# A gated convolution and state-space block on eight cores: the recurrence scanned over chunks of eight tokens, the convolution as banded products, and orders from a list scheduler

## The chip, the cores and the metric

The kernel runs on all 8 cores of one Trainium2 chip, one batch element per core. The metric is the device time of the slowest core, in microseconds (us). Some executions fall into a slower state, in which the cores of one die show a lower granted TensorE clock than those of the other (in the slowest run of e12, 2099.60 us, 0.803 against 0.969); such runs are called slow and are left out of every comparison. Several chips were used, so each changed kernel was timed in turns with the kernel before on the same chip.

Names: TensorE (PE in the profile) does matrix products, VectorE (DVE) and ScalarE (ACT) do elementwise work, and the DMA queues are issued by SyncE (SP) and GpSimd (POOL). PEld in the profile is the loading of a matrix into TensorE. "ps" names the banks of PSUM, the memory into which TensorE writes its sums. A table load (ACT_TABLE_LOAD) is an instruction in ScalarE's queue, 1283 ns each; it stands between some pairs of ScalarE functions and not between others. An eviction is the operation that takes a finished sum out of PSUM.

## The reference, cut to what matters

x is 8 x 2048 x 2048; 16 meta tokens are put in front, so each core works on 2064 tokens of width 2048. E is 1024.

```python
xn = rmsnorm(h)                                    # over 2048 channels
v, g, z_c, u, z_s, gl_c, gl_s = split(xn @ w_in)   # widths E,E,E,E,E,2048,2048
# convolution branch
a = v * sigmoid(g)
a = causal_depthwise_conv(a, width=31) + dw_b
y_c = silu(layernorm(a)) * silu(z_c)               # layer norm over the E channels
# state-space branch: 64 groups of 16 channels, 64 complex states per group
s[t] = lam_bar * s[t-1] + B_bar @ u[t]             # complex, diagonal lam_bar
y_s = gelu(real(C @ s) + d_skip * u)
y_s = y_s * sigmoid(y_s @ w_glu + b_glu) * silu(z_s)
# gated merge
m = sigmoid(gl_c + b) * (y_c @ w_conv) + sigmoid(gl_s + b) * (y_s @ w_ssm)
out = rmsnorm(h + m @ w_out)
```

Layer norm needs all 1024 channels of the convolution, and the products with `w_conv`, `w_ssm` and `w_out` come after both branches.

## The kernel before

Weights and activations are in bf16, sums in fp32. The text of the program is the order of each engine's queue; waits on semaphores are derived from the buffers that an operation reads and writes. A Python generator interleaves the recurrence with the projections by hand.

The recurrence works token by token on 512 tokens at a time, with two groups' 64 states on the 128 partitions. The complex state is turned into two real scans: the input is modulated by cosine and sine tables, scanned with a real decay, and demodulated again. All of that is VectorE's work (`S5ENG` is VectorE).

```python
# per pair of groups and tile of 512 tokens; f[0..3] are quarters of P and Q   (cut)
mm(ps[pr][:, 0:w], BT[rp:rp + 32, 0, blk, :], ub, ...)            # real part of B u
mm(ps[pi_][:, 0:w], BT[rp:rp + 32, 1, blk, :], ub, ...)           # imaginary part
tt("dve", Pv, psW, ecb, ALU.mult, ...)                            # modulation, 1024 wide
tt("dve", Qv, psW, esb, ALU.mult, ...)                            # modulation, 1024 wide
tt(S5ENG, f[0][:, 0:w], f[0][:, 0:w], f[1][:, 0:w], ALU.add, ...)
tt(S5ENG, f[2][:, 0:w], f[2][:, 0:w], f[3][:, 0:w], ALU.subtract, ...)
# ... two scans of 512, real and imaginary: tensor_tensor_scan(mult, add)
tt("dve", TT_["P"]..., SQ, ecb, ALU.mult, ...)                    # demodulation, 1024 wide
tt("dve", TT_["Q"]..., SQ, esb, ALU.mult, ...)                    # demodulation, 1024 wide
# ... then four products with C and one with the skip matrix on TensorE
```

The convolution has 23 of its 31 taps on TensorE, as products with diagonal matrices, and 8 taps on VectorE:

```python
for k in range(NDT, CW):                 # NDT = 8, CW = 31
    mm(ps[bk][:, 0:w], DG[m % 2][:, k - NDT, :], ABUF2[:, m, t0 + k:t0 + k + w], ...)
# ...
for k in range(1, NDT):
    for ai_, (t0, w) in enumerate(pair_tiles):
        stt(cacc[ai_][:, 0:w], ABUF2[:, m, t0 + k:t0 + k + w], dww_t[:, m, k:k + 1],
            cacc[ai_][:, 0:w], ALU.mult, ALU.add, ...)
```

Of the kernel before, what the change touches and what calls it, by code (L numbers as in the profile page):

```python
# [10 lines left out]
I32 = mybir.dt.int32  # L11
# [10 lines left out]
PADL = CW - 1  # L22
NORM_EPS = 1e-6
LN_EPS = 1e-5
SMW = 4352
# [4 lines left out]
TT_ALL = [(0, NM)] + [(NM + 512 * i, 512) for i in range(4)]  # L30
TT_REAL = TT_ALL[1:]

C_V, C_G, C_ZC, C_U, C_ZS, C_GLC, C_GLS = 0, 1024, 2048, 3072, 4096, 5120, 7168

SAME_ENGINE_WAITS = ("pool", "act", "dve")
S5ENG = "dve"

class _Stop(Exception):
    pass

class Src:
    def __init__(self, sem, step):
        self.sem, self.step, self.count = sem, step, 0

class Buf:
    __slots__ = ("w", "r")

    def __init__(self):
        self.w = None
        self.r = []  # L50

def alias_from(new_bufs, old_bufs):
    evs = []
    for b in old_bufs:
        if b.w is not None:
            evs.append(b.w)
        evs.extend(b.r)
    for nb in new_bufs:
        nb.r = list(nb.r) + evs

class Sched:
    def __init__(self):
        self.eng = {}

    def add_engine(self, name, sem):
        self.eng[name] = dict(src=Src(sem, 1), insts=[], waited={})

    def op(self, eng, fn, reads=(), writes=(), signal=True, src=None):
        En = self.eng[eng]
        s = src if src is not None else En["src"]  # L70
        need = {}
        srcs = {}
        deps = []
        for b in reads:
            if b.w is not None:
                deps.append(b.w)
        for b in writes:
            if b.w is not None:
                deps.append(b.w)
            deps.extend(b.r)  # L80
        for (ds, v) in deps:
            if ds is En["src"] and (eng == "pe" or eng not in SAME_ENGINE_WAITS):
                continue
            k = id(ds)
            if v > need.get(k, 0):
                need[k] = v
                srcs[k] = ds
        waits = []
        for k, v in need.items():
            if En["waited"].get(k, 0) >= v:  # L90
                continue
            En["waited"][k] = v
            waits.append((srcs[k].sem, v))
        if signal:
            s.count += s.step
            ev = (s, s.count)
            sig = (s.sem, s.step)
        else:
            ev = (s, s.count + s.step)
            sig = None  # L100
        En["insts"].append((waits, fn, sig))
        for b in reads:
            b.r.append(ev)
        for b in writes:
            b.w = ev
            b.r = []
        return ev

    def wait_all(self, eng, events):
        En = self.eng[eng]  # L110
        waits = []
        for (ds, v) in events:
            k = id(ds)
            if En["waited"].get(k, 0) >= v:
                continue
            En["waited"][k] = v
            waits.append((ds.sem, v))
        En["insts"].append((waits, None, None))

    def emit(self, name, e):  # L120
        for waits, fn, sig in self.eng[name]["insts"]:
            for sem, v in waits:
                e.wait_ge(sem, v)
            if fn is None:
                continue
            ins = fn(e)
            if sig is not None:
                ins.then_inc(sig[0], sig[1])

def build(dbg=None):  # L130
    nc = bass.Bass("TRN2", target_bir_lowering=False)
    S = Sched()
# [7 lines left out]
    w_in = din("w_in", [D, 9216])  # L140
    b_gate = din("b_gate", [4096])
    dw_w = din("dw_w", [CW, 1, E])
    dw_b = din("dw_b", [E])
    ln_g = din("ln_g", [E])
    ln_b = din("ln_b", [E])
    w_conv = din("w_conv", [E, D])
    lam_re = din("lam_re", [64, 64])
    lam_im = din("lam_im", [64, 64])
    log_step = din("log_step", [64])
    b_re = din("b_re", [64, 64, 16])  # L150
    b_im = din("b_im", [64, 64, 16])
    c_re = din("c_re", [64, 16, 64])
    c_im = din("c_im", [64, 16, 64])
    d_skip = din("d_skip", [E])
    w_glu = din("w_glu", [E, E])
    b_glu = din("b_glu", [E])
    w_ssm = din("w_ssm", [E, D])
    w_out = din("w_out", [D, D])
    final_g = din("final_g", [D])
    out = nc.dram_tensor("out", [SEQ, D], F32, kind="ExternalOutput").ap()  # L160
    ps_scr = nc.dram_tensor("ps_scr", [64, 128, L], BF16).ap()
    dbg_out = None
    if dbg is not None:
        dbg_out = nc.dram_tensor("dbg", list(dbg["shape"]), F32, kind="ExternalOutput").ap()

    es = ExitStack()
    with es:
        def sb(name, shape, dt):
            return es.enter_context(nc.sbuf_tensor(name, list(shape), dt))

        def sem(name):
            return es.enter_context(nc.semaphore(name))

        XM = sb("XM", [128, 16, L], BF16)
        AC = sb("AC", [128, 33264], BF16)
        WS = sb("WS", [128, 4, 4096], BF16)
        TA = sb("TA", [128, 8192], BF16)
        SM = sb("SM", [128, SMW], F32)
        ident = sb("ident", [128, 128], BF16)
        identf = sb("identf", [128, 128], F32)  # L180
        ones_b = sb("ones_b", [128, 128], BF16)
        BT = sb("BT", [128, 2, 8, 128], BF16)
        WC = sb("WC", [128, 3, 8, 128], BF16)
        DSKD = sb("DSKD", [128, 8, 128], BF16)
        ps2 = [es.enter_context(nc.psum_tensor(f"ps{i}", [128, 1024], F32)) for i in range(4)]
        ps = [ps2[j // 2][:, (j % 2) * 512:(j % 2 + 1) * 512] for j in range(8)]
        psB = [Buf() for _ in range(8)]

        A_EL = 8 * (L + PADL)
        Aap = AC[:, 0:A_EL]  # L190
        Cap = AC[:, A_EL:A_EL + 8 * L]
        ABUF = Aap.rearrange("p (b t) -> p b t", b=8)
        UBUF = ABUF[:, :, PADL:]
        CBUF = Cap.rearrange("p (b t) -> p b t", b=8)
        A_f32 = Aap.bitcast(F32)
        C_f32 = Cap.bitcast(F32)
        AC_f32 = AC[:, :].bitcast(F32)

        for n in ("pe", "act", "dve", "pool", "sp"):
            S.add_engine(n, sem("s_" + n))  # L200

        def dsrc(name):
            return Src(sem(name), 16)

        XMB = [[Buf() for _ in range(5)] for _ in range(16)]

        def tidx(t0):
            return 0 if t0 < NM else 1 + (t0 - NM) // 512

        def xm_all(k):  # L210
            return tuple(XMB[k])
        WSb = [Buf() for _ in range(4)]
        Ab = [Buf() for _ in range(8)]
        Cb = [Buf() for _ in range(8)]
        TAb = Buf()
        SMb = Buf()
        CONSTb = Buf()
        S5Wb = Buf()

        sm_off = [0]  # L220

        def smalloc(n):
            o = sm_off[0]
            sm_off[0] += n
            assert sm_off[0] <= SMW - 1024, sm_off[0]
            return SM[:, o:o + n]

        def act(out_, in_, func, bias=0.0, scale=1.0, accum=None, reads=(), writes=()):
            if accum is None:
                return S.op("act", lambda e: e.activation(out=out_, in_=in_, func=func, bias=bias, scale=scale),  # L230
                            reads, writes)
            return S.op("act", lambda e: e.activation(out=out_, in_=in_, func=func, bias=bias, scale=scale,  # L232
                                                      accum_out=accum), reads, writes)

        def tt(eng, out_, in0, in1, op, reads=(), writes=()):
            return S.op(eng, lambda e: e.tensor_tensor(out=out_, in0=in0, in1=in1, op=op), reads, writes)  # L236

        def ts(eng, out_, in0, s1, s2, op0, op1=None, reads=(), writes=()):
            if op1 is None:
                return S.op(eng, lambda e: e.tensor_scalar(out=out_, in0=in0, scalar1=s1, scalar2=None, op0=op0),  # L240
                            reads, writes)
            return S.op(eng, lambda e: e.tensor_scalar(out=out_, in0=in0, scalar1=s1, scalar2=s2, op0=op0, op1=op1),
                        reads, writes)

        def stt(out_, in0, scalar, in1, op0, op1, reads=(), writes=()):
            return S.op("dve", lambda e: e.scalar_tensor_tensor(out=out_, in0=in0, scalar=scalar, in1=in1,  # L246
                                                                op0=op0, op1=op1), reads, writes)

        def cp(eng, out_, in_, reads=(), writes=()):
            if eng == "act":  # L250
                return S.op("act", lambda e: e.copy(out=out_, in_=in_), reads, writes)  # L251
# [975 lines left out]
```

## Time and profile before

The kernel before took 2489.11 us (median of three runs, 2469.27 to 2709.86; the highest is a slow one).

| Reading | Value |
|---|---|
| span of the profiled core | 2464.5 us |
| TensorE busy | 2035.2 us (83%), 9368 matmuls |
| VectorE busy | 1732.1 us (70%) |
| ScalarE busy | 779.3 us (32%), 61 table loads |

The first view of the kernel before is the table by stages: the window in us and its length, then the busy time of each engine with its number of instructions, the granted TensorE clock (1.00 is full), the share of time in which the DMA engines were busy, and what they moved in GB/s.

```profile
core 2: us, PE busy (x) PEld busy (x) DVE busy (x) ACT busy (x) POOL busy (x), PEclk, DMA share, GB/s
0.00:246.00 246.00, 91.31 (x659) 56.04 (x660) 54.94 (x56) 64.77 (x93) 23.39 (x27) 0.89 0.61 96
246.00:400.00 154.00, 99.01 (x437) 44.32 (x435) 56.77 (x137) 42.75 (x98) 5.39 (x6) 0.79 0.19 24
400.00:1500.00 1100.00, 1074.62 (x4985) 437.73 (x4984) 1076.38 (x1468) 476.83 (x725) 33.11 (x29) 0.98 0.31 57
1500.00:1660.00 160.00, 108.28 (x444) 44.37 (x442) 58.97 (x65) 55.04 (x100) 1.18 (x2) 0.82 0.22 57
1660.00:1870.00 210.00, 174.09 (x748) 74.69 (x749) 194.35 (x297) 61.88 (x146) 1.75 (x2) 0.93 0.19 55
1870.00:2050.00 180.00, 122.08 (x471) 49.48 (x469) 123.22 (x177) 41.45 (x44) 4.38 (x5) 0.81 0.36 86
2050.00:2464.50 414.50, 365.80 (x1633) 161.21 (x1630) 167.51 (x218) 36.58 (x49) 7.88 (x9) 0.92 0.48 128
```

The middle stage, 400 to 1500 us, holds the recurrence and most projections. TensorE and VectorE are both about 98% busy there. The stages around it (start, 1500 to 1660, 1870 to 2050) leave TensorE idle for 155, 52 and 58 us.

The second view of the kernel before is TensorE's list of waits: what it waited for, in us in total, how often, and the longest.

```profile
PE ps L262 <- DVE AC L246: 148.4, 17, 28.7
PE ps L256 <- DVE XM L236: 70.3, 13, 23.8
PE ps L256 <- DMA AC<-w_out: 38.4, 8, 19.9
...
```

Its first line is the normalised x: TensorE waits for VectorE at the start. The third view, of the same kernel, is the chain of waits that ended last (start, duration, what); it shows the rate of dense matmuls of 512 columns, 7.01/32 = 219 ns and 210.42/968 = 217 ns.

```profile
391.18 7.01 PE ps L256 x32
...
2243.81 210.42 PE ps L256 x968
```

The fourth view of the kernel before is VectorE's groups by line and shape (busy us, mean ns of one). With the groups cut here (additions 166.1, the second scan 161.0, the other demodulation 98.9), modulation, demodulation, scans and taps make 1250 of VectorE's 1732 us.

```profile
L236 DVE TENSOR_TENSOR AC<-ps,TA 128x1024 f32<-128x1024 f32 x256 | 307.7, 1209 | 11.2 <-PE ps L258 11.0
L236 DVE TENSOR_TENSOR AC<-AC,TA 128x1024 bf16<-128x1024 f32 x172 | 202.5, 1218 | 0.1
...
L719 DVE TENSOR_TENSOR_SCAN AC<-SM,AC 128x512 f32<-128x512 f32 x128 | 163.8, 1280 | 6.5
...
L246 DVE SCALAR_TENSOR_TENSOR XM<-XM,SM 128x512 f32<-128x512 bf16 x224 | 149.7, 745 | 0.0
```

### The profile page before, as it was taken

Reading aid. Unit: us, or ns where it says so; the run is one execution under the profiler, and the core shown is the slowest. Engines: PE = TensorE matmul, PEld = TensorE weight load, DVE = VectorE, ACT = ScalarE, POOL = GpSimd, SP = SyncE. Lnnn points to the kernel's source line nnn. Section 1 sums busy time; section 2 is a strip of 40 time slices with the busy share of each in tenths; the row PEclk is TensorE's granted clock in tenths of the full one; section 3 lists DMA queues with packets and bytes.
Section 4 is the critical chain, followed back from the end, with each engine's and each line's share of the span. In section 5 each row is a group of like instructions: output and inputs, shape, how many; then the busy total and the mean of one; then the engine's idle time right before and its main releaser. Section 6 shows DMA issues by size and latency. Waiting matters only on the chain.

```text
span 2464.5 us, 27461 instructions; the slowest of 8 cores (2447.9 to 2464.5 us)
## 1 busy us (share of the span) xinstructions
PE 2035.2 (83%) x9368; PEld 867.8 (35%) x9368; DVE 1732.1 (70%) x2416; ACT 779.3 (32%) x1253; POOL 77.1 (3%) x80
## 2 busy tenths in 40 slices
PE   1056829998998999999999999558887749958998
PEld 1033414433333334444444444223333214423443
DVE  2122039999999999999999999129996767622333
ACT  3122133244443444535444443342323210001111
POOL 2100000000000000000000000000000000010000
PEclk9987959999999999999999999779988879977999
DMA  9831042323232323333233320231111264267444
GB/s 190 50 90 52 1 52 43 69 45 60 35 61 44 61 59 54 69 61 67 45 69 69 60 52 26 43 110 62 35 38 31 87 135 109 72 120 142 161 147 137
DMA packets 120953, 179.45 MB, mean 73 GB/s; under 512 B 6593, under 2 KB 96705, under 8 KB 114400
## 3 DMA queue, kind: packets, MB, share of 16 engines
q0 software_dynamic: 92848, 57.89, 20.4%
q1 hardware_dynamic: 27968, 119.81, 14.4%
q8 instruction: 77, 1.26, 0.2%
q14 instruction: 60, 0.49, 0.1%
HBM read 183.91 MB, written 50.40 MB: 95 GB/s over the span
## 4 chain that ended last, share of the span: by engine, by line
PE 67%; DVE 12%; DMA 8%; issue 8%; ACT 3%; another core or an unknown queue 1%; POOL 0%; DVEq 0%; SPq 0%; ACTq 0%; POOLq 0%
PE ps L256 59%; PE ps L258 7%; DVE AC L236 4%; DMA WS<-w_in 2%; DMA AC<-w_out 2%; DVE XM L236 2%; DMA AC<-x 1%; DVE AC L722 1%; DVE AC L246 1%; DMA TA<-ps_scr 1%; ACT TA L232 1%; DVE SM L236 1%; DMA WS<-ps_scr 1%; DVE AC L719 1%
## 5 line engine op out<-in xcount | busy, mean ns | idle before, releaser
L256 PE MATMUL ps<-XM,WS 128*128 128x512 bf16 (+1 forms) x4992 | 1047.5, 367 | 14.6 <-DMA WS<-w_in 6.3
L256 PEld LDWEIGHTS ps<-XM,WS 128*128 128x128 bf16 x4992 | 453.3, 99 | 591.0 <-issue 91.2
L256 PE MATMUL ps<-AC,WS 128*128 128x512 bf16 x1280 | 299.5, 399 | 80.5 <-DMA WS<-w_conv 30.5
L236 DVE TENSOR_TENSOR AC<-ps,TA 128x1024 f32<-128x1024 f32 (+1 forms) x320 | 316.1, 1002 | 14.2 <-PE ps L258 11.0
L256 PE MATMUL ps<-AC,XM 128*128 128x512 bf16 x1024 | 234.6, 393 | 38.4 <-DMA AC<-w_out 38.4
L236 DVE TENSOR_TENSOR AC<-AC 128x512 f32<-128x512 f32 (+2 forms) x326 | 183.4, 603 | 76.5 <-ACT AC L230 76.2
L256 PEld LDWEIGHTS ps<-AC,WS 128*128 128x128 bf16 x1280 | 129.3, 102 | 251.0 <-issue 115.6
L256 PE MATMUL ps<-XM,TA 128*128 128x512 bf16 x736 | 170.8, 395 | 51.7 <-DVE XM L236 51.7
L236 DVE TENSOR_TENSOR AC<-AC,TA 128x1024 bf16<-128x1024 f32 x172 | 202.5, 1218 | 0.1
L719 DVE TENSOR_TENSOR_SCAN AC<-SM,AC 128x512 f32<-128x512 f32 (+1 forms) x160 | 169.9, 1062 | 9.2
L230 ACT ACTIVATE WS<-ps,SM 128x512 bf16<-128x512 f32 x128 | 87.9, 687 | 264.8 <-PE ps L256 264.6
L722 DVE TENSOR_TENSOR_SCAN AC<-SM,AC 128x512 f32<-128x512 f32 (+1 forms) x160 | 166.4, 1040 | 0.0
L232 ACT ACTIVATE TA<-WS 128x2048 bf16<-128x2048 f32 x16 | 30.6, 1910 | 421.7 <-DVE WS L236 421.7
L230 ACT ACTIVATE WS<-ps 128x512 bf16<-128x512 f32 x128 | 76.3, 596 | 276.2 <-PE ps L256 264.4
L256 PEld LDWEIGHTS ps<-AC,XM 128*128 128x128 bf16 x1024 | 101.9, 100 | 171.0 <-issue 57.4
L262 PE MATMUL ps<-ident,AC 128*128 128x128 bf16 (+1 forms) x272 | 30.4, 301 | 148.4 <-DVE AC L246 148.4
L236 DVE TENSOR_TENSOR WS<-ps,WS 128x512 f32<-128x512 f32 x64 | 44.2, 690 | 151.1 <-PE ps L256 150.8
L246 DVE SCALAR_TENSOR_TENSOR XM<-XM,SM 128x512 f32<-128x512 bf16 x224 | 149.7, 745 | 0.0
L251 ACT CAST AC<-ps 32x512 bf16<-32x512 f32 (+2 forms) x168 | 93.6, 558 | 170.9 <-PE ps L256 103.5
L256 PEld LDWEIGHTS ps<-XM,TA 128*128 128x128 bf16 x736 | 73.3, 100 | 149.2 <-issue 69.4
L427 DVE RECIPROCAL SM<-SM 128x1 f32<-128x1 f32 (+1 forms) x17 | 2.8, 163 | 149.3 <-ACT SM L230 149.3
L230 ACT ACTIVATE TA<-ident,SM 128x128 bf16<-128x128 bf16 x184 | 73.7, 401 | 107.3 <-PE ps L256 91.0
(103 smaller groups left out, 1519.5 us busy)
## 6 DMA issues: line engine op xcount, KB each, us to landing
WS<-w_in POOLq DMA_DIRECT2D x36, 1024.0 KB, 13.1
ps_scr<-WS SPq DMA_DIRECT2D x64, 512.0 KB, 3.1
AC<-x SPq DMA_DIRECT2D x16, 1024.0 KB, 9.3
TA<-ps_scr SPq DMA_DIRECT2D x32, 512.0 KB, 3.6
WS<-x SPq DMA_DIRECT2D x16, 1024.0 KB, 8.2
out<-WS SPq DMA_DIRECT2D x16, 1024.0 KB, 5.9
WS<-ps_scr SPq DMA_DIRECT2D x16, 516.0 KB, 5.8
WS<-ps_scr SPq DMA_DIRECT2D x16, 512.0 KB, 5.4
```

The lines of the kernel that those rows point to most:

```text
L230: return S.op("act", lambda e: e.activation(out=out_, in_=in_, func=func, bias=bias, scale=scale), reads, writes)
L232: return S.op("act", lambda e: e.activation(out=out_, in_=in_, func=func, bias=bias, scale=scale, accum_out=accum), reads, writes)
L236: return S.op(eng, lambda e: e.tensor_tensor(out=out_, in0=in0, in1=in1, op=op), reads, writes)
L246: return S.op("dve", lambda e: e.scalar_tensor_tensor(out=out_, in0=in0, scalar=scalar, in1=in1, op0=op0, op1=op1), reads, writes)
L251: return S.op("act", lambda e: e.copy(out=out_, in_=in_), reads, writes)
L256: return S.op("pe", lambda e: e.matmul(out_, lhsT, rhs, start=start, stop=stop), reads, writes, signal=signal)
L258: return S.op("pe", lambda e: e.matmul(out_, lhsT, rhs, start=start, stop=stop, tile_position=tile_position), reads, writes, signal=signal)
L262: return S.op("pe", lambda e: e.transpose(out_, in_, idn), reads, writes, signal=signal)
L427: S.op("dve", lambda e, rows=rows, s=s: e.reciprocal(out=rst[0:rows, s:s + 1], in_=ssq[0:rows, s:s + 1]), (stB[s],), (stB[s],))
L719: S.op("dve", lambda e: e.tensor_tensor_scan(out=f[3][:, 0:w], data0=rq.broadcast_to([128, w]), data1=f[0][:, 0:w], initial=ini_re, op0=AL ...
L722: S.op("dve", lambda e: e.tensor_tensor_scan(out=f[1][:, 0:w], data0=rq.broadcast_to([128, w]), data1=f[2][:, 0:w], initial=ini_im, op0=AL ...
```

## The change

The intent is to take work from VectorE and TensorE by treating 8 tokens as one chunk. Inside a chunk, the recurrence is a product with a small matrix; only the state at the chunk's borders is scanned, 257 columns instead of 2064. The same order of the tokens (by place in the chunk, then by chunk) makes the depthwise convolution five products per group of 16 channels with banded matrices of 128 x 128. To bring tokens into that order, u, a, y and the convolution's result travel through scratch in device memory. The constants (powers of the decay, matrices) are computed on the chip at the start. The hand-made interleaving goes: every operation is given a priority and an estimated duration, and a list scheduler orders each engine's queue before the program is emitted. The core of the diff, with cuts:

```diff
+    def schedule(self, bw=220e3):
+        # ... at each step the engine that is free first takes, of its ready operations,
+        # the one with the smallest priority number; durations are a model
+        _, _, o = heapq.heappop(rdy[e])
+        free[e] = t + o.dur
...
-                tt("dve", Pv, psW, ecb, ALU.mult, ...)        # 1024 wide, and Q likewise
-                tt(S5ENG, f[0][:, 0:w], ...)                  # and f[2]
-                # two scans of 512, two demodulations of 1024
+            for gp in range(4):
+                # tables of 257 columns for two groups (VectorE and ScalarE)
+                for gg in range(2):
+                    mms([(pv[:, 0, 0:257], V3[:, g, :], u3[:, g, 0:257], True, True),
+                         (pv[:, 1, 0:257], Vs3[:, g, :], u3[:, g, 0:257], True, True)], 257, ...)
+                    tt(t3, pv[:, :, 0:257], t4[:, gg, :, :], ALU.mult, n=514, ...)
+                    tt(v_, t3[:, 0, :], t3[:, 1, :], ALU.add, n=257, ...)
+                    S.op("dve", lambda e: e.tensor_tensor_scan(out=x_, data0=mag8..., data1=v_, ...), 0.65, ...)
+                    tt(d3, x_[:, 1:257]..., t4[:, gg, :, 1:257], ALU.mult, n=512, ...)
+                    mms([(yo, Lo3[:, g, :], u3[:, g, 2:258], True, False),
+                         (yo, C3[:, g, 16:144], d3[:, 0, :], False, False),
+                         (yo, Cs3[:, g, :], d3[:, 1, :], False, True)], 256, ...)
...
-                        for k in range(NDT, CW):
-                            mm(ps[bk][:, 0:w], DG[m % 2][:, k - NDT, :], ...)
-                    # 8 taps on VectorE
+            for q in range(2):
+                tz, tzB = TZ[q]
+                dma("pool", [(tz, w_dw[2 * m + q])], ...)
+                        mms([(ps[bk][:, gg * 256:gg * 256 + 256], z4[:, gl, d, :], a3[:, g, 4 - d:260 - d], d == 0, d == 4)
+                             for d in range(5)], 256, ...)
...
+        gg = [tile("ST", o_x + i * 8192, 8192) for i in range(2)]     # sigmoid of the gated linear unit
+        mean = [tile("ST", o_x + n * 2048, 2048, F32) for n in range(4)]      # same bytes
```

The last two lines are not neighbours in the program. "Gated linear unit" (GLU) means the product of y_s with `w_glu`, its sigmoid and what follows.

## The prediction

> **What bounds it now.** TensorE: the chain that ended last is 67% TensorE. In the middle stage (400 to 1500 us, table by stage) it is 92 to 100% busy at a granted clock near 1.00; the chain lists 32 matmuls of 512 columns in 7.01 us, 219 ns each, and in the output stage 968 in 210.4, 217 ns. [...] in the first 246 us TensorE is busy for 91 (the waits name VectorE's normalise, 148.4); from 1540 to 2010 VectorE leads with convolution taps (149.7), layer norm and gates; 38.4 go to w_out. In the middle stage VectorE is 97% busy too.
>
> **What the change does.**
> - TensorE: 8416 matmuls[...]. Recurrence 1024 matmuls down to 320 of half width; convolution 736 down to 320 of half width. The large products stay.
> - VectorE: scans of 512 (325 us), modulation (308), demodulation (301), adds (166), taps (150) go. In come, for each of 64 groups, a product of 514 from PSUM (0.69), an add of 257 (0.42), a scan of 257 (0.66), a product of 512 (0.69), half a table (1.0): 223 us; matrices 96 x 0.72 = 69. So 290 instead of 1250.
> - ScalarE: silu and sine alternate in the old trace without a table load; I expect tanh to join them, so loads fall far below 61.
> - DMA: gate weights are read twice, but 3 MB per 21 us of matmuls is well below w_out's 16.8 MB in 55.8 us. The tiny parameter reads[...] go.
>
> **Where it lies.** TensorE's time by stage: until the u projection ends 150 us (35 idle; x takes 9.3 us per MB, three buffers); v/g 225; z 224; recurrence 47; convolution 35; waits there for VectorE, about as loaded as TensorE, whose durations the scheduler underrates by some 10%: 30; a hand-over of 110, then GLU 56; gates and branches 3072 x 0.218 = 670; output 223; last waits and tail 16. Sum about 1790.
>
> The hand-over is the one large hole: GLU's sigmoid buffers lie on the mean and rstd buffers, so GLU stops after three PSUM banks until layer norm is done: convolution scratch out and in (about 7 us), four squares of 3.6 with column sums (22), then 32 x three products of 0.69 (66).
>
> **Predicted: 1795 us, 8 in 10 between 1720 and 1885.** Chances: faster by over 2% 0.98, within 0.01, slower 0.01.
>
> **What would show it.** TensorE busy above 88%, chain mostly TensorE at 217 to 219 ns; under 60 us of TensorE idle before u is done; one hole of 70 to 110 us with VectorE busy, before the GLU matmuls; short waits on VectorE in the recurrence; no DMA wait in the gate stage; under 25 table loads; VectorE busy below 850 us.
>
> **What would make it wrong.** The orders are fixed from modelled durations: if real ones slip, in-order queues (604 DMA issues on one) block each other and the recurrence stage stretches by 50 to 100 us. [...]If the layer-norm hole is hidden, about 1710.

Where a cut is marked, the passage rested on something that no trace of this case shows: a formula for the time of a matmul and the total times that were worked out with it, a cause for the late first weights of the kernel before, and a cause for a lowered clock. The terms come to 1786 us (150 + 225 + 224 + 47 + 35 + 30 + 110 + 56 + 670 + 223 + 16), and the forecast was set at 1795. Its matmul terms can be followed from the measured 217 to 219 ns for 512 columns (1024 of them make 224 us; 320 of half width, at half of that, make 35). The durations of single operations of VectorE in it are estimates; what was measured stands under "VectorE's work" below.

## The result, and the profile after

The changed kernel took 1873.34 us (median of four runs, 1871.32 to 1878.11), against 2479.79 us for the median of four runs of the kernel before. The ratio is 0.7579 with a 95% interval of 0.7547 to 0.7611. In the experiments below, a ratio is the mean time of one kernel's fast runs over that of the other's fast runs of the same rounds, so it is not quite the ratio of the medians quoted. All eight cores agree (1841.1 to 1870.0 us, clock 0.950 to 0.958).

| Reading | Before | After |
|---|---|---|
| span | 2464.5 us | 1870.0 us |
| TensorE busy | 2035.2 us (83%) | 1640.9 us (88%) |
| VectorE busy | 1732.1 us (70%) | 694.4 us (37%) |
| ScalarE busy, table loads | 779.3 us, 61 | 509.0 us, 25 |
| matmuls by the instruction lists | 9368 | 8416 |
| span less TensorE's busy time | 429.3 us | 229.1 us |

So, of the 594 us by which the span fell, 394 are TensorE's busy time (2035.2 - 1640.9) and 200 are time in which it had stood still (429.3 - 229.1). How much of the 394 is matmuls that no longer exist, and how much a difference in the granted clock, was not separated. The table by stages of the kernel after, with the columns as before:

```profile
0.00:228.00 228.00, 147.01 (x975) 88.23 (x976) 122.65 (x211) 88.52 (x140) 5.15 (x17) 0.91 0.56 142
228.00:550.00 322.00, 321.64 (x1945) 183.66 (x1944) 251.72 (x507) 125.99 (x202) 6.82 (x13) 0.99 0.45 90
550.00:781.60 231.60, 212.11 (x1105) 108.90 (x1105) 0.00 (x0) 78.88 (x126) 10.70 (x21) 0.96 0.78 168
781.60:956.00 174.40, 82.22 (x322) 33.88 (x327) 93.47 (x144) 77.35 (x87) 1.06 (x2) 0.73 0.18 54
956.00:1621.80 665.80, 655.19 (x2988) 297.81 (x3042) 137.62 (x203) 87.72 (x128) 36.51 (x64) 0.99 0.46 85
1621.80:1870.00 248.20, 222.74 (x1005) 100.66 (x1023) 88.92 (x130) 50.53 (x145) 0.00 (x0) 0.95 0.45 143
```

The windows are: until the u projection ends; v, g and the recurrence; the z projections and the convolution; the hand-over through layer norm and the gated linear unit; gates and branch products; output. TensorE is near 100% busy in the second and fifth. VectorE is idle, 0.00 us, in the whole third, and then works 93 us in the fourth while TensorE waits. TensorE's list of waits in the kernel after:

```profile
PE ps L327 <- ACT ST L294: 56.7, 11, 27.9
PE ps L327 <- DVE CY L301: 42.1, 3, 37.8
PE ps L333 <- DVE CY L312: 35.6, 5, 26.1
PE ps L333 <- DVE ST L301: 21.0, 1, 21.0
PE ps L327 <- DMA XM<-w_out: 14.4, 1, 14.4
PE ps L327 <- DMA CY<-c_scr: 11.6, 1, 11.6
PE ps L327 <- DMA ST<-u_scr: 8.5, 1, 8.5
PE ps L327 <- DMA WS<-w_main: 7.7, 1, 7.7
```

Two places hold most of them. At the start, lines L333 (transposes of x) wait for the normalised x. In the hand-over, L327 waits for layer norm (DVE CY L301) and for ScalarE's evictions (ACT ST L294). The chain of waits of the kernel after, at the start:

```profile
6.11 40.62 DMA CY<-par
...
47.49 2.35 DVE CY L312
49.98 1.88 PE ps L333 x16
```

The load of the parameter table takes until 46.7 us. VectorE's queue is in order, and operations on those parameters stand in it ahead of the normalise of the next x tile (L312); they wait 12.6 and 4.4 us for their loads, so x waits for parameters that the x tile does not need. In the third stage, TensorE's time line of the kernel after shows when the convolution's products run (start us, duration; twenty matmuls are one half of a block of 128 channels) and when layer norm's column sums can begin:

```profile
586.00 2.35 PE L327 MATMUL ps<-ST 128*128 128x256 bf16 x20
595.10 2.35 PE L327 MATMUL ps<-ST 128*128 128x256 bf16 x20
...
779.36 2.35 PE L327 MATMUL ps<-ST 128*128 128x256 bf16 x20
...
793.29 5.55 PE L327 MATMUL ps<-CY,ones_b 128*128 128x512 bf16 x16 [11.58 <-DMA CY<-c_scr]
```

The sixteen half blocks start between 554.67 and 779.36 us, 15 us apart on average ((779.36 - 554.67)/15), though each has only 2.35 us of matmuls. The last eviction of z is sent at 774.7 us: the convolution ends when the projections that could cover its successor are over.

Its start is held too. The buffers of the banded matrices lie on bytes that the recurrence uses (`TZ` and `gt` to `gd`, both at `o_t` in the program). GpSimd's time line shows that the first load of banded matrices waited for the recurrence's last scan (L780):

```profile
545.49 0.53 POOL L339 DMA_DIRECT2D ST<-w_dw  x1 [26.94 <-DVE ST L780]
```

### The profile page after: what moved, and what is told of

It is laid out like the page before. It is cut to its first block, busy times and chain, and to the rows that moved or that the text cites. A ratio compares the mean times of both kernels' runs of the same rounds, so it can differ in the third digit from the quotient of the medians.

```text
span 1870.0 us, 22995 instructions; the slowest of 8 cores (1841.1 to 1870.0 us)
## 1 busy us (share of the span) xinstructions
PE 1640.9 (88%) x8333; PEld 813.1 (43%) x8416; DVE 694.4 (37%) x1193; ACT 509.0 (27%) x826; POOL 60.2 (3%) x116
## 3 DMA queue, kind: packets, MB, share of 16 engines
q1 hardware_dynamic: 89504, 107.91, 19.5%
## 4 chain that ended last, share of the span: by engine, by line
PE 81%; DMA 8%; DVE 4%; issue 4%; ACT 2%; SPq 1%; DVEq 0%; ACTq 0%; POOLq 0%
PE ps L327 80%; DMA XM<-w_out 2%; DMA CY<-par 2%; DMA WS<-w_main 2%; DVE ST L301 1%; ACT ST L294 1%; DVE CY L301 1%; PE ps L333 1%; DMA CY<-y_scr 1%; DVE CY L312 1%; ACT L294 1%; DMA ST<-u_scr 1%; SPq L339 1%; ACT CY L294 0%; DMA CY<-c_scr 0%
## 5 line engine op out<-in xcount | busy, mean ns | idle before, releaser
L327 PE MATMUL ps<-XM,WS 128*128 128x512 bf16 (+5 forms) x4992 | 1049.1, 368 | 38.8 <-ACT ST L294 18.7
L327 PEld LDWEIGHTS ps<-XM,WS 128*128 128x128 bf16 x4992 | 491.1, 99 | 546.4 <-issue 57.6
L327 PE MATMUL ps<-CY,WS 128*128 128x512 bf16 x1218 | 288.3, 384 | 74.4 <-DVE CY L301 42.1
L294 ACT ACTIVATE ST<-ps,SM 128x512 f32<-128x512 f32 (+2 forms) x224 | 140.0, 627 | 684.7 <-PE ps L327 680.3
L301 DVE TENSOR_TENSOR ST<-ps,ST 128x512 f32<-128x512 f32 x128 | 88.5, 692 | 522.1 <-PE ps L327 509.2
L327 PEld LDWEIGHTS ps<-CY,WS 128*128 128x128 bf16 x1280 | 126.3, 99 | 227.7 <-issue 81.0
L301 DVE TENSOR_TENSOR ST<-ST 128x257 f32<-128x257 f32 (+3 forms) x160 | 85.4, 546 | 256.5 <-ACT ST L914 249.9
L294 ACT ACTIVATE ST<-ps 128x512 bf16<-128x512 f32 (+2 forms) x104 | 57.9, 566 | 171.5 <-PE ps L327 170.7
L294 ACT ACTIVATE CY<-CY 128x514 f32<-128x514 f32 (+2 forms) x74 | 56.6, 782 | 67.8 <-DVE CY L312 51.8
L333 PE MATMUL ps<-ident,CY 128*128 128x128 bf16 (+1 forms) x272 | 21.5, 242 | 60.1 <-DVE CY L312 35.6
L327 PE MATMUL ps<-XM,ST 128*128 128x512 bf16 x250 | 58.8, 390 | 14.9 <-DMA XM<-w_out 14.4
L327 PE MATMUL ps<-ST,CY 128*128 128x256 bf16 (+1 forms) x320 | 51.8, 276 | 8.9 <-DMA ST<-u_scr 8.5
L312 DVE SCALAR_TENSOR_TENSOR CY<-CY,SM,ST 128x2048 bf16<-128x2048 f32 (+2 forms) x25 | 58.6, 2349 | 1.9
L327 PE MATMUL ps<-CY,XM 128*128 128x512 bf16 x252 | 56.3, 379 | 0.2
L327 PE MATMUL ps<-CY,ST 128*128 128x512 bf16 x252 | 56.3, 379 | 0.2
L327 PE MATMUL ps<-XM 128*128 128x512 bf16 x250 | 56.1, 379 | 0.3
L301 DVE TENSOR_TENSOR ST<-ps,CY 128x514 f32<-128x514 f32 x64 | 42.5, 685 | 34.3 <-PE ps L327 21.1
L301 DVE TENSOR_TENSOR WS<-ps,WS 128x512 f32<-128x512 f32 x32 | 21.6, 690 | 83.9 <-PE ps L327 82.5
L333 PEld LDWEIGHTS ps<-ident,CY 128*128 128x128 bf16 (+1 forms) x272 | 19.3, 111 | 63.2 <-issue 61.4
```

Source lines behind the costliest of these rows:

```text
L294: f = lambda e: e.activation(out=out_, in_=in_, func=func, bias=bias, scale=scale)
L301: return S.op(eng, lambda e: e.tensor_tensor(out=out_, in0=in0, in1=in1, op=op), d, reads, writes, **kw)
L312: return S.op("dve", lambda e: e.scalar_tensor_tensor(out=out_, in0=in0, scalar=scalar, in1=in1, op0=op0, op1=op1), 0.12 + n / 960.0, read ...
L327: return lambda e: e.matmul(a[0], a[1], a[2], start=a[3], stop=a[4])
L333: return lambda e: e.transpose(a[0], a[1], a[2])
```

## The experiments

Twelve kernels ran. Each ran beside the kernel before, so they can be read against each other through their ratios. In the diffs, names are those of the program. Line numbers in the profiles differ by a few between kernels, because the edits move lines.

### Buffers of the gated linear unit moved (e1_glu)

Theory: the sigmoid's buffers lie on layer norm's mean and rstd, so the gated linear unit cannot run under layer norm. Rival: layer norm's own work sets the length of the hand-over.

```diff
-        gg = [tile("ST", o_x + i * 8192, 8192) for i in range(2)]
+        gg = [tile("WS", 24576, 8192), tile("ST", 0, 8192)]
```

> The changed kernel with one edit: the two GLU sigmoid buffers lie in a free weight slot and in the idle staging area, no longer on the mean and rstd buffers. Theory (the hole before GLU is a buffer conflict): TensorE waits 92 us between the last convolution product at 781.6 us and the steady GLU products at 906 us; the 56 us of GLU products move into it, and up to 28 us of gate products follow into free banks, so the time falls by 40 to 65 us to 1805 to 1830 us. Rival (the hole is layer norm itself, its data and VectorE's work): GLU goes earlier, the same hole opens after it, before the branch products, and the time stays within 10 us of 1870.

Measured: 1853.95 us median, one slow run of 2048.74; ratio 0.7506 [0.7492, 0.7519]. That is 19 us less than after, between the two. TensorE's waits between 776 and 960 us, in this kernel:

```profile
PE ps L327 <- ACT ST L294: 35.7, 10, 22.6
PE ps L327 <- DVE CY L301: 25.0, 4, 9.9
...
```

With two smaller ones they sum to 64 us, against 92 in the kernel after for the same window (42.1 + 38.0 + 11.6 + 0.2). The products did move under layer norm, but part of the wait came back. Table loads rose from 25 to 55, as ScalarE now alternates between the sigmoid of the gated linear unit and the silu of layer norm; what that costs is tested in e11. Neither theory holds alone.

### The constants held until x is normalised (e2_setup)

```diff
+        if prio == 20 and eng in ("dve", "act") and self.hold:   # prio 20: constants
+            after = list(after) + self.hold
...
+        S.hold = [o for o in S.ops if o.prio == 2]               # all x-tile operations
```

> The changed kernel with one edit: VectorE and ScalarE work that prepares the recurrence's constants may not start before the last x tile has been normalised and transposed. Theory (in-order queues: constants stand ahead of x tiles and of u evictions because the scheduler thought their parameters would be there sooner): the u projection ends 35 to 50 us earlier than its 228 us, the wait of VectorE for parameters at 29 to 47 us goes, and the time falls by 30 to 45 us to 1825 to 1840. Rival (the start is bound by the 14 MB that land in the first 47 us, not by order): u ends within 10 us of 228 and the time stays within 10 us of 1870. Third possibility: u ends earlier but the recurrence starts later, the convolution is pushed past the z projection, and the gain is given back there.

Measured: 1853.47 us, ratio 0.7506 [0.7492, 0.7519]: 20 us less than after. The u projection ended at 204 us instead of 228, and the wait for parameters went. Both are less than the theory expected (35 to 50 us for u, 30 to 45 for the time). What is left is x itself: in the first 50 us the DMA engines were 97% busy at 225 GB/s (the rival's 14 MB do not fit the trace of the kernel after, where 9.9 MB were moved in the first 47 us, at 210 GB/s), and after that the x tiles came out one per 5.3 us, as each passes ScalarE, VectorE and TensorE in order. So the order of VectorE's queue explains 24 of the 78 us that the start cost more than predicted.

### Program order instead of the scheduler's (e3_prog)

```diff
         S.schedule()
+        S.log = [(0.0, o) for o in S.ops]
```

> The changed kernel with every queue in program order instead of the list scheduler's order; the work is the same. Theory (the redesign pays only because the scheduler lays the recurrence, 337 us long in the trace, and the convolution under the projections): both come out in the open, TensorE's matmul time stays near 1640, and the time is 2200 to 2350 us, most of the way back to the kernel before. Rival (queues that run ahead of each other give the overlap by themselves): below 2050 us.

Measured: 2688.93 us (2688.39 the median of the fast runs), ratio 1.0877 [1.0858, 1.0897]: slower than the kernel before, and worse than expected. TensorE's waits in this kernel:

```profile
PE ps L327 <- DVE ST L301: 259.3, 64, 5.6
PE ps L327 <- DMA ST<-a_scr: 168.7, 8, 44.6
...
PE ps L327 <- DMA ST<-u_scr: 115.1, 8, 15.3
...
```

The table by stages of the same kernel, with the columns as before:

```profile
400.00:800.00 400.00, 71.43 (x340) 32.88 (x340) 207.26 (x388) 76.68 (x119) 0.00 (x0) 0.50 0.12 20
```

With nothing between them, each of the 64 groups makes TensorE wait for VectorE, and each of the 8 blocks waits for a round trip through scratch. TensorE is 18% busy from 400 to 800 us and its granted clock there is 0.50. So, for this program text, the order is worth 815 us (2688 - 1873). This is not the gain over the kernel before, whose text was interleaved by hand.

### Each scan issued twice (e4_scan2)

```diff
                     S.op("dve", lambda e: e.tensor_tensor_scan(...), 0.65, (vB, mag8B), (xB,), prio=10)
+                    S.op("dve", lambda e: e.tensor_tensor_scan(...), 0.65, (vB, mag8B), (xB,), prio=10)
```

> The changed kernel with each of the 64 scans of 257 done twice (the second overwrites the first with the same values); adds 64 x 0.66 = 42 us to VectorE, which is 77 to 84% busy in the recurrence stage, and the scheduler knows of it. Theory (VectorE no longer limits that stage; TensorE waits for it there for under 1 us): the time grows by less than 12 us. Rival (VectorE is as loaded as TensorE, as my prediction had it): it grows by 25 to 45 us.

Measured: 1879.23 us, ratio 0.7602 [0.7589, 0.7615], about 6 us more than after, for 42.6 us of additional scans on VectorE. TensorE showed no wait at all between 220 and 550 us. VectorE does not limit TensorE in the recurrence stage. The recurrence itself did end later: the first load of banded matrices was sent at 580.26 us instead of 545.49. But the convolution's products then took 187 us from first to last (603.2 to 789.8) instead of 227 (554.7 to 781.7), so only 8 us of the delay were left at their end.

### The gelu held until the last z is evicted (e5_gelu)

```diff
+                ZL = act(pt, ps[bk], AF.Silu, ...)             # eviction of z
-            act(YS_t[m][0], YS_t[m][0], AF.Gelu_apprx_tanh, ..., prio=16)
+            act(YS_t[m][0], YS_t[m][0], AF.Gelu_apprx_tanh, ..., prio=16, after=(ZL,))
```

> The changed kernel with one edit: the eight gelu passes wait for the last z eviction instead of lying between the evictions of the convolution stage. Theory (ScalarE, in order, stands still at a gelu that waits for its scratch reload, and loads a table on each side, so z evictions come late and TensorE waits 19 us in the stage 555 to 735 us): those waits fall below 5 us, table loads fall from 25 to 8 to 12, and the time falls by 10 to 20 us. Rival (the waits only move: 8 x 1.91 us of gelu now stand ahead of layer norm's squares in the hand-over): the time stays within 6 us of 1870 and the hand-over is 10 to 17 us longer.

Measured: 1863.95 us, ratio 0.7546 [0.7534, 0.7558], 9.4 us less. Table loads fell from 25 to 14. Waits for ScalarE's evictions under the z projections fell from 18.7 to 12.6 us, but a new one of 18.9 us for the gelu itself appeared behind the last of them. A part of the gain was given back: the time is just under the theory's 10 to 20 us, and neither its waits (below 5 us) nor its table loads (8 to 12) were met.

### The recurrence taken out, after and before (e6_nos5, e7_b_nos5)

Both give a wrong result; u goes through in y's place.

```diff
-            y2, y2B = Y2[m % 2]
-            for gp in range(4):
+            y2, y2B = u2, u2B
+            for gp in range(0):
...
-            s5_mats(m)                                       # the matrices, too
```

> The changed kernel without the recurrence (wrong result on purpose: y is u; the rearranging transfers, gelu, GLU and the constants stay). Theory (the recurrence now costs only its matmuls and a little more, being hidden under the projections): 320 products of 257 or 256 columns (35 us), the small ones that build matrices (12) and the wait of 8.5 go, so 45 to 75 us less, 1798 to 1828. Rival (it still sets the pace of its stage through VectorE or ScalarE): over 100 us less.

> The kernel before without the recurrence (wrong result on purpose: y is u; gelu and projections stay). Its stage from 246 to 1540 us would hold only 4096 + 384 projection matmuls, 910 to 930 us. Theory (the old recurrence cost its 1024 matmuls and the waits it put between them): 340 to 400 us less, 2070 to 2130 us. With the run without the recurrence on the changed kernel this gives the recurrence's share of the 609 us won: 280 to 350. Rival (the projections alone are bound by two PSUM banks and ScalarE): less than 250 us less.

In the kernel before, the table generation, both scans, modulation, demodulation, additions and the small products of all 160 steps are taken out in the same way.

Measured: after without recurrence 1742.93 us, ratio 0.7044 [0.7027, 0.7061], 130 us less than after; before without recurrence 2181.68 us, ratio 0.8827 [0.8810, 0.8845], 291 us less than the fast runs of before in the same rounds. Both miss what the theory expected. For the kernel after, the rival's number (over 100 us) was met, but not its reason: between 228 and 550 us TensorE had waited for VectorE for 0.4 us only. The kernel after pays far more than the recurrence's matmuls: TensorE's busy time fell by only 62 us (1640.9 to 1578.5), so 68 of the 130 us are waits. Where they were is shown together with the next pair.

### The convolution taken out, after and before (e8_noconv, e9_b_noconv)

Their outputs are wrong, which doesn't matter for the times. The gated value goes on in place of the convolution's result.

```diff
-            for q in range(2):            # load of the banded matrices, products, eviction
+            for q in range(0):
...
-            dma("sp", [(cd[j], c3[16 * j:16 * j + 16, :, :]) for j in range(8)], ...)
+            dma("sp", [(cd[j], a3[16 * j:16 * j + 16, :, 4:260]) for j in range(8)], ...)
```

> The changed kernel with the convolution's banded products and their eviction taken out: the gated value itself goes through the scratch in its place (wrong on purpose). Theory: convolution costs the new kernel its 35 us of matmuls and most of the 31 us that TensorE waited between 550 and 800 us, beside the products: 1795 to 1835 us, 40 to 80 less than after. Rival: it costs only its matmuls or less, because the hand-over behind it stays where it was: 1840 to 1870 us.

> The kernel before with the convolution taken out, taps and products both; the gated value is copied into the place of its result (wrong on purpose). Theory: most of its stage (1663 to 1870 us, of which 171 us are matmuls) goes: 2270 to 2320 us, 150 to 200 less than before. So the change would have won some 110 to 150 us of its gain by the convolution. Rival: the stage is mostly cover for work on VectorE and ScalarE that stays: 2370 us or more, under 100 saved.

Measured: after without convolution 1759.86 us, ratio 0.7123 [0.7107, 0.7138], 113 us less than after. This is more than either theory said. The edit also takes out the sixteen loads of banded matrices (640 KB each), so it does not part the products from their loads. Before without convolution 2290.2 us in its two fast runs (two were slow, 2366.68 and 2437.50), ratio 0.9274 [0.9251, 0.9297], 179 us less than before, as the theory said.

The kernel after loses 113 us with 49 us of TensorE's busy time taken away (1640.9 to 1591.8; the convolution's matmuls themselves take 37.5), and 130 us with 62 us. The same waits explain both. TensorE's time line shows the first column sums of layer norm, in the kernel without recurrence:

```profile
570.58 3.40 PE L327 MATMUL ps<-CY,ones_b 128*128 128x512 bf16 x15
```

and in the kernel without convolution:

```profile
675.11 3.40 PE L327 MATMUL ps<-CY,ones_b 128*128 128x512 bf16 x15
```

They begin 153 us (723.7 - 570.6) and 69 us (744.3 - 675.1) before the last z is sent off, where the kernel after begins them 19 us behind it (793.3 against 774.7). Layer norm then runs under the z projections, and the hand-over shrinks. From 228 us to about the first gate products TensorE stands still for 112 us in the kernel after (to 956 us), for 46 us in the kernel without recurrence (to 830 us) and for 51 us in the one without convolution (to 850 us).

Without the recurrence the convolution also starts earlier. Its half blocks begin 196 us before those of the kernel after (358.17 against 554.67), and the last of them ends at 546.3:

```profile
358.17 4.54 PE L327 MATMUL ps<-ST 128*128 128x256 bf16 x40
...
543.99 2.35 PE L327 MATMUL ps<-ST 128*128 128x256 bf16 x20
```

So removing either part lets layer norm start early, and both removals get back much the same waits. Their savings should not be added; no run took out both.

### Three mends together (e10_four)

The mends of e1, e2 and e5 in one kernel. The gates' evictions also get buffers off layer norm's:

```diff
-        gst = [tile("ST", 32768 + i * 2048, 2048, F32) for i in range(4)]
+        gst = [tile("WS", 24576 + i * 2048, 2048, F32) for i in range(4)]
```

> The changed kernel with the edits of e1, e2 and e5 together, and the gate buffers moved out of layer norm's way as well, so that the gate stage may start on finished halves. The three alone gave 19, 20 and 10 us. If they are independent, 1815 to 1830 us; if the gate buffers were what held the rest of the hand-over, 1785 to 1810; if ScalarE's table loads (54 of them in e1) hold it, no better than 1825.

Measured: 1825.79 us, ratio 0.7387 [0.7374, 0.7400], 47.5 us less than after; the three gains alone sum to 49. They add up, and the fourth move adds nothing that shows.

### The sigmoid of the gated linear unit as a tanh (e11_tanh)

```diff
-                act(g3[:, m, :], ps[bk], AF.Sigmoid, bias=PAR["bglu"][:, m:m + 1], ...)
+                act(g3[:, m, :], ps[bk], AF.Tanh, bias=hbg[:, m:m + 1], scale=0.5, ...)      # hbg = bglu / 2
-                tt(YSv..., YSv..., g3[:, m, :], ALU.mult, ...)
+                stt(YSv..., g3[:, m, :], 1.0, YSv..., ALU.add, ALU.mult, ...)
-                        tt(g_, ps[bk], g_, ALU.mult, ...)
+                        stt(g_, ps[bk], 1.0 - 0.5 * br_, g_, ALU.mult, ALU.mult, ...)
```

> The kernel of the three mends together (1825.8 us), with the sigmoid of the gated linear unit computed as a tanh, which shares a table with silu (half of the scaled input, then one added in the product, the factor of a half in the last product of the branch); result right. Theory: what the moved buffers did not win was lost to table loads, which alternated 55 times; they fall below 20 and the hand-over loses 20 to 40 us more: 1785 to 1805 us. Rival: layer norm's own 64 units on VectorE, about 2.1 us each, set the length of the hand-over, and the products now cost VectorE 10 us more than before: within 10 us of 1825.8.

Measured: 1814.3 us as the median of its four fast runs (1840.03 is slow), ratio 0.7347 [0.7332, 0.7363]: 10 to 11 us less than e10, at the rival's edge and half of what the theory expected. Table loads fell from 46 to 30, not below 20. ScalarE's time line in this kernel, within layer norm:

```profile
842.23 1.51 ACT L297 ACTIVATE ST<-ST,SM 128x512 f32<-128x512 f32 x2
843.76 0.69 ACT L297 ACTIVATE ST<-ps,SM 128x512 bf16<-128x512 f32 x1
...
866.95 0.69 ACT L297 ACTIVATE WS<-ps,SM 128x512 f32<-128x512 f32 x1
867.65 1.28 ACT L297 ACT_TABLE_LOAD   x1
868.95 0.81 ACT L297 ACTIVATE ST<-ST,SM 128x512 f32<-128x512 f32 x1
869.78 1.28 ACT L297 ACT_TABLE_LOAD   x1
871.08 0.69 ACT L297 ACTIVATE WS<-ps,SM 128x512 f32<-128x512 f32 x1
```

At 842 us the silu of layer norm (ST from ST) and the tanh of the gated linear unit (ST from ps) follow each other without a load. From 865 us on, the sigmoid of the first gates (WS from ps) takes the place of the old sigmoid, and the alternation is back. So table loads were a part of what e1 could not win. How much more the gates' sigmoid is worth was not run. VectorE was busy for 25 of the 30 us from 835 to 865, so there layer norm's own work is close to being the limit.

### The loads of the output stage (e12_tail)

```diff
-                (WOB[n],), prio=34)
+                (WOB[n],), prio=34, after=(GD[1, 3 + 5 * n],) if n < 2 else ())
...
-        FIRST = 4
+        FIRST = 6
```

> The kernel of the run before this one, with two changes to the loads of the output stage: six row blocks instead of four are computed against the first half of the output matrix before its second half is asked for, and the first half's two loads are held until the fourth and the ninth gate tile of the second half of the tokens are done. Result right. Theory: TensorE's two waits on loads (16.2 us for the output matrix, 9.6 us for a gate weight that lands behind it) go: 20 to 26 us less than the run before. Rival: the second half only gets free with the last gate, the loads of x share its bandwidth, and the wait moves to another load: under 8 us less.

Measured: 1789.02 and 1789.46 us in the two fast runs (1947.90 and 2099.60 are slow: one die at clock 0.88 or 0.80); ratio 0.7246 [0.7228, 0.7263]. That is 25 us less than e11 on the same chip, as the theory said. The list of TensorE's waits from 1000 us on is empty in this kernel. Its list of waits over the whole span begins with the largest:

```profile
PE ps L336 <- DVE CY L315: 43.6, 6, 23.4
PE ps L330 <- DVE CY L304: 27.2, 2, 24.0
...
```

This kernel, with a right result, is 4.5% faster than the kernel after. What is left is the start (L336 waits for the normalised x) and layer norm.

## Why the prediction was right or wrong

The time was predicted at 1795 us with a range of 1720 to 1885, and came at 1873.34, inside the range and 78 us above the middle. Nearly all of that comes from one term of the sum. Against the stages of the profile:

| Term of the prediction | Predicted us | Measured us | Difference |
|---|---|---|---|
| until the u projection ends | 150 | 228.0 | +78 |
| v/g 225, z 224, recurrence 47, convolution 35, waits 30 | 561 | 553.6 | -7 |
| hand-over 110, gated linear unit 56 | 166 | 174.4 | +8 |
| gates and branches | 670 | 665.8 | -4 |
| output 223, waits and tail 16 | 239 | 248.2 | +9 |
| sum | 1786 | 1870.0 | +84 |

**The matmuls: count and rate right.** 8416 matmuls were predicted, and 8416 ran; TensorE was busy for 1640.9 us. Dense stages ran at 217 to 219 ns for 512 columns (968 in 210.42 us in the kernel before, 49 in 10.74 us in the gate stage of the kernel after), and the chain is 81% TensorE. The granted clock was 0.99 in the two densest stages of the kernel after (228 to 550 and 956 to 1621.8 us), and the means of the eight cores over their spans were 0.950 to 0.958. In slow runs the mean of one die's cores was lower: 0.803 in the slowest run of e12, 0.845 in that of e1. TensorE's share, 87.7%, is just short of the "above 88%" that was predicted.

**VectorE's work: right.** 694.4 us busy, under the 850 predicted. The estimates for single operations held: the recurrence's product of 512 took 683 ns, where 0.69 had been taken, and a scan of 257 took 682 ns against 0.66. The 128 fp32 products of 512 in the gates took 692 ns. A scan of 512 columns in fp32 took 1258 to 1280 ns in the kernel before, so a scan took about 2.3 ns per additional column ((1269 - 682)/255), against 1.05 for an addition in fp32 (687 ns at 512, 420 ns at 257).

**The start: mis-sized, and the step that failed is "until the u projection ends 150 us (35 idle ...)".** TensorE waited 81.0 us in this stage instead of 35, which is 46 of the 78. Transposes of x took 22 us of TensorE that the sum left out, and the 639 matmuls of u took 124.7 us instead of the 115 left over for them, about 10 more. The argument had also said that the tiny parameter reads of the kernel before would go (the first weights landed there up to 49.3 us after they were issued; what held them was not shown). They did go, but a large parameter load came in their place and held the chain to 46.7 us, through the order of VectorE's queue. The second experiment shows that 24 us hang on that order (228 to 204). The rest lies in the load of x, at 97% busy DMA engines, and in the chain of each x tile; it was not separated further.

**Waits for VectorE in the recurrence: wrong in place, and nil in size.** 30 us were predicted; the trace shows 0.4 between 228 and 550 us, and doubling every scan cost 6 us. VectorE was busy for 78% of that stage (251.7 of 322 us), not "about as loaded as TensorE". In their place stood 19.5 us of waits in the z stage (231.60 - 212.11), mostly for ScalarE, which loaded a table on each side of a gelu or a row of gelus. The total came out right by luck, because one error covered the other.

**The hand-over: right in size, half right in cause.** A hole of 70 to 110 us was predicted and 92 us were found. The shared buffers were named as the reason that the gated linear unit could not fill it. Moving them won 19 us, so they were one of three causes. The second is table loads between sigmoid and silu (e11). The third the prediction did not see: it costed the convolution at 35 us of matmuls and took for granted that it would be done early. It is a chain of sixteen short groups of products 15 us apart. It could not start before the recurrence had left the shared buffers, at 545 us, and it ends only with the z projections, so layer norm has nothing left to hide under. The two kernels with a part taken out show it, with column sums that begin 153 and 69 us before the last z is sent.

**Gates and output: right, with small loads missed.** "No DMA wait in the gate stage" was wrong by one wait of 7.7 us, for a weight that landed behind the output matrix; 14.4 us for the second half of the output matrix came near what was predicted as last waits. The twelfth kernel took both away.

**Table loads: at the border.** "Under 25" was predicted and exactly 25 were found. That silu and sine alternate without a load is shown by the kernel before (no load between 309.34 and 507.91 us); that tanh joins sine by the kernel after (both run between 159.33 and 536.07 us, without a load), and that it joins silu by e11 (842.23 to 844.45 us). A load cost its 1283 ns and hardly more: in e11 an activation ended at 867.64, a load between sigmoid and silu ran from 867.65 to 868.93, and the next activation began at 868.95.

**Where the gain of 600 us came from.** The recurrence costs 291 us in the kernel before and 130 in the kernel after, the convolution 179 and 113. The differences are 161 and 66 us. Since savings can overlap within a kernel, and no run took out both parts, it is not shown how much of the other 370 us or so lies outside these two. By the accounts of the span the gain is 394 us of TensorE's busy time and 200 us of its idle time. That the scheduler is needed is shown, as without it the new program is slower than the old one.

**Open.** What paces the convolution was not tried. It is no fixed pace: the same sixteen half blocks took 227 us in the kernel after, 187 us with the scans doubled (e4) and 188 us without the recurrence (358.2 to 546.3). In its stage the DMA engines were 78% busy, and GpSimd's queue waited 105 us for TensorE to free the two buffers of banded matrices, whose loads take a median of 9.0 us; but TensorE itself waited only 0.7 us for such a load, so its products came where the scheduler's order had put them. Buffers that the recurrence does not share, or more of them, would tell. Nor was the start tried with smaller first loads.

## What to carry to other kernels

Cost a new stage by the length of its chain (load, product, eviction, scratch out and in) and by what must wait for its last piece, not only by its busy time: 37.5 us of matmuls were strung out over 227 us, and in the kernel without them layer norm's column sums begin 118 us earlier (675.1 against 793.3). When a part is taken out to see what it costs, the waits that vanish may belong to a hole that several parts share, so such savings do not add. With in-order queues, look at the start for work that nobody needs yet: constants that stand ahead of x cost 20 us here, and holding them back took a few lines.
